# All low parts of a stage by accumulating transfers, and a third modulation computed as rows, in a two-layer trunk kernel

## Chip, core and metric

The kernel runs on one core of one Trainium2 chip. The metric is the device time of one execution in microseconds (us). Before the change three runs gave 1405.65, 1405.88 and 1407.29, median 1405.88. The execution whose trace is shown took 1407.28, and its span, from the first to the last instruction, is 1405.5.

The engines are called as the profile calls them: PE (TensorE, matmuls), DVE (VectorE), ACT (ScalarE), POOL (GpSimd) and SP (SyncE, which issues most transfers). Each works through its own list of instructions in a fixed order.

## What is computed

Two layers of a "hybrid gated parallel" block with width 1024 over 256 latent and 256 context tokens; layer 0 does both sets (512 columns), layer 1 only the latents, with keys and values of the context. In short:

```python
ml = silu(c) @ w_ada + b_ada          # six vectors of 1024: shift, scale, gate, shift, scale, gate
z  = modulate(x, ml[0], ml[1]) @ w_in + b_in
m  = sig(g0)*attention(q, k, v) + sig(g1)*conformer_conv(a) + sig(g2)*multiscale_pool(p)
x  = layer_norm(ALPHA*x + ml[2]*(m @ w_out + b_out))
x  = layer_norm(ALPHA*x + ml[5]*conv_ffn(modulate(x, ml[3], ml[4])))
```

`conformer_conv` is a gated linear unit, a depthwise convolution of 31 taps over the tokens, a layer norm, a silu and a pointwise matmul ("pw"). The vector `ml[2]` of layer 0, called modulation (0,2), is needed only behind the pointwise matmul, at `m @ w_out`.

## The kernel before

**Matmuls.** Activations lie with channels on partitions and tokens (512) in the free dimension. Each fp32 operand is split into a high part, rounded to the type fp32r, and a low part, the rest. Each product is three matmuls, high by high, low by high, high by low (lines 438, 439 and 440 of the program). One weight chunk (128 by 1024 fp32, 512 KB) gives eight slices of the contraction, so 24 matmuls of 512 columns into one accumulator bank. Four PSUM banks ("mm") are for these, three ("ax") for transposes and attention, one ("ad") for the modulation on PE.

**Weights.** They stream from memory in a fixed order, `ORDER`. SP loads a chunk into one of five buffers `raw`, or one of three buffers `rawt`. ACT copies it to `hi` (L290). The low part `lo` is made in one of two ways: DVE subtracts, `raw - hi` (L298), or, for the chunks in the list `SUMMED`, ACT writes minus `hi` into `lo` (L292) and POOL issues a transfer that adds the weights from memory to it (L294). Five chunks can be held as `hi` and `lo`. `SUMMED` holds every other chunk of layer 0's gates, pools and pointwise matmul, 22 of 44.

**Stages of layer 0.** Convolution inputs, keys and values, queries (two halves; the second half ends in four banks at once, which DVE empties into `nat` with the bias `bq`, L937), then sixteen steps of gates, pools, and attention heads spread over them, about 189 to 435 us; then the pointwise chunks. For each half of the queries DVE rotates `nat` to `rot` (POOL makes one part of it, `rotb`, and `rq`, the norm's factor), PE transposes, ACT and DVE split the result into `qThi` and `qTlo` (L449). A head's scores go through row maximum `mx` (L973), its product `nb`, exponential on ACT `p`, and PE transposes.

**Taps.** The depthwise convolution is 30 operations on DVE per block of channels (L796 on `H`), eight blocks. They are handed out in lots: `NTAPS` gives the lot for each phase (in the gate steps 10 in layer 0), and from step `FLUSH` on all that are left. They have a lower priority than other work. The finished `H` are transposed on PE (L505), their statistics taken, and normalized (`nat`, L529 and L533); after the gates they are transposed back (L544) and go through silu to `ch` and `clo`, the operands of the pointwise matmul.

**Modulations.** Two ways again. Kind "ada": PE multiplies eight chunks by `silu(c)` (L364, eight matmuls to a chunk as the trace counts them), DVE adds the bias (L371), and the row goes to memory. Kind "adt": the chunk lies in a `rawt` buffer, transposed, and DVE multiplies and sums it against the broadcast `silu(c)`, one pass for the latents and one for the context (L396), into a column of `mods`. A taken "adt" chunk is put on a list, `due`; `run_due(2)` at the end of each of the sixteen steps emits two. In layer 0's gates stage (0,2) is of the first kind, (0,4) and (0,3) of the second.

**Order.** A list scheduler, with a model of its own, orders each engine's instructions when the program is built. Where a line says `keep_in_program_order`, the instruction only stays behind the last such one of its engine. So the order that results is not that of the program text, and is shown below.

Of the kernel before, what the change touches and what calls it, by code (L numbers as in the profile page):

```python
# [7 lines left out]
F32 = mybir.dt.float32  # L8
# [5 lines left out]
P = 128  # L14
DEPTH = 2
D = 1024
KT = 8
# [24 lines left out]
NFF = 3  # L42
S3 = (1, 0)
PV3 = (0, 0)
FLUSH = (13, 14)
LATER = 1
HEAD_AT = (0, 1, 2, 4, 5, 7, 9, 10)
MIX_AT = 4
GRP = 3
GATES = ((0, 2), (0, 5), (1, 2), (1, 5))  # L50
TAPS_LATER = 60
NTAPS = ((10, 6, 10, 1000), (12, 7, 11, 1000))

_VEC = [
    ("b_in", 60), ("b_ada", 48), ("dw_b", 8), ("cln_g", 8), ("cln_b", 8), ("pw_b", 8),
# [8 lines left out]
NV = _o  # L64


_ADA = {(0, "mix"): ((0, 2),), (0, "up"): ((0, 5),), (1, "conv"): ((1, 2),), (1, "up"): ((1, 5),)}

_ADT = {(0, "mix"): ((0, 4), (0, 3)), (0, "up"): ((1, 1),), (0, "down"): ((1, 0), (1, 4), (1, 3))}

PRE = [("conv", 1, j, h) for j in range(8) for h in range(2)] + [("kv", 1, k) for k in range(4)]
PRE += [("q", 1, c, k) for c in range(2) for k in range(4)]
# [4 lines left out]
def _spread(main, extra):  # L77

    res, n = [], 0
    for i, x in enumerate(main):  # L80
        res.append(x)
        while n < len(extra) and n * len(main) < (i + 1) * len(extra):
            res.append(extra[n])
            n += 1
    return res


def weight_order(l):

    o = [("conv", l, j, h) for j in range(8) for h in range(2)]  # L90
    o += [("kv", l, k2) for k2 in range(4)]
    o += [("q", l, c, k2) for c in range(2) for k2 in range(4)]
    for n in range(16):
        b, i = (("g0", "g2", "pool")[n % 3], n // 3) if n < 12 else ("g1", n - 12)
        o += [(b, l, 2 * i), (b, l, 2 * i + 1)]
        if n >= MIX_AT and (n - MIX_AT) % 3 == 0 and n - MIX_AT < 12:
            o.append(("plw", l, (n - MIX_AT) // 3))
    o += [("pw", l, c) for c in range(8)]
    ada = {
        ph: [("ada", a, m, k) for a, m in _ADA.get((l, ph), ()) for k in range(KT)] for ph in ("mix", "conv", "up")  # L100
    }
    adt = {ph: [("adt", a, m, c) for a, m in _ADT.get((l, ph), ()) for c in range(KT)] for ph in ("mix", "up", "down")}

    o = o[:GRP] + ada["conv"] + o[GRP:20] + _spread(o[20:], _spread(ada["mix"], adt["mix"]) if l == 0 else [])
    o += [("wout", 0, h, p) for h in range(2) for p in range(4)] if l == 0 else [("wout", 1, k) for k in range(KT)]
    up = [("up", l, j, h) for j in range(FT) for h in range(2)]
    o += up[:GRP] + ada["up"] + _spread(up[GRP:], _spread([("pre",) + it for it in PRE if l == 0], adt["up"]))
    if l == 0:
        down = [("down", 0, h, p) for h in range(2) for p in range(FT // 2)]
        o += _spread(down[:-HOLD - 2], adt["down"]) + down[-HOLD - 2:]  # L110
    else:
        o += [("down", 1, k) for k in range(FT)]
    return o
# [23 lines left out]


SUMMED = [it for it in weight_order(0) if it[0] in ("g0", "g1", "g2", "pool", "plw", "pw")]
SUMMED = [it for i, it in enumerate(SUMMED) if i % 2]  # L140

OFFSET, _o = {}, 0
for _it in ORDER:
# [7 lines left out]
def trunk(ctx: ExitStack, tc: tile.TileContext, xT, xn, cT, crow, wst, vec, brow, grow, rows, bgate, rope, icnt, ident, out):  # L151
    nc = tc.nc
    V, A, G, PE, SP = nc.vector, nc.scalar, nc.gpsimd, nc.tensor, nc.sync
# [5 lines left out]
    dp = ctx.enter_context(tc.tile_pool(name="dp", bufs=1, space=bass.MemoryType.DRAM))  # L159
# [6 lines left out]
    def uid(name):  # L166
        cnt[0] += 1
        return f"{name}{cnt[0]}"
# [25 lines left out]
    def aux():  # L194
        return pax.tile([P, 512], F32, tag="ax", name=uid("ax"))

    def sm(w, name, bufs=None):
        return st.tile([P, w], F32, tag=f"sm_{name}", name=uid(name), bufs=bufs)
# [102 lines left out]
    def take(it):  # L301

        while True:
            i = nxt["use"]
            nxt["use"] += 1
            load_to(i + (LA0 if strict else LA))
            split_to(i if strict or only else ahead[i])
            if ORDER[i][0] not in ("ada", "adt", "pre") and unfinished:
                unfinished[0][0] -= 1
                if not unfinished[0][0]:  # L310
                    unfinished.pop(0)[1]()
            if ORDER[i] == it:
                return raw.pop(it) if it[0] == "ad0" else split.pop(it)
            if ORDER[i][0] == "ada":
                ada(*ORDER[i][1:])
            elif ORDER[i][0] in ("adt", "pre"):
                due.append(ORDER[i])
# [22 lines left out]
    mods = {}  # L340
    ada_ps = {}
    gate_row = {}
# [44 lines left out]
    def adt(l, m, c):  # L387

        w = raw.pop(("adt", l, m, c))
        n = 2 if l == 0 or m < 2 else 1  # L390
        if c == 0:
            mods[l, m] = const.tile([P, KT, 2], F32, name=f"mod{l}_{m}")
            if n == 1:
                G.memset(mods[l, m], 0.0)
        for s in range(n):
            tc.keep_in_program_order(V.tensor_tensor_reduce(  # L396
                prod, w, cb[:, s], 1.0, col(l, "b_ada", m * 8 + c), ALU.mult, ALU.add, mods[l, m][:, c, s:s + 1],
            ))

    def run_due(n):  # L400

        for _ in range(min(n, len(due))):
            it = due.pop(0)
            (adt if it[0] == "adt" else pre)(*it[1:])
# [75 lines left out]
    def mmB(w, src, T, ps=None, s=None):  # L480

        ps = mmb() if ps is None else ps
        a, b = (0, T) if s is None else (s * SEQ, (s + 1) * SEQ)
        mm3(ps[:, a:b], [(part(w, k * P, (k + 1) * P), part(src[k], a, b)) for k in range(len(src))])
        return ps
# [278 lines left out]
    for l in range(DEPTH):  # L764
# [278 lines left out]

        def gates(b, c):
            gate_end(b, c, mmB(take((f"g{b}", l, c)), hT, T))

        def gate_end(b, c, ps):
            g = ST(T, name=f"g{b}")
            A.activation(g[:, :T], ps[:, :T], AF.Sigmoid, bias=col(l, "b_in", 36 + 8 * b + c))
            gate[b, c] = g  # L1050
# [5 lines left out]
        def pooled(g):  # L1056
            w = 2 << g
            res = []
            for c2 in range(2):
                ps = mmB(take(("pool", l, 2 * g + c2)), hT, T)  # L1060
                u = mp.tile([P, 2, 272], F32, tag="pu", name=uid("pu"), bufs=2)
                V.memset(u[:, :ns, 0:8], 0.0)
                V.memset(u[:, :ns, 264:272], 0.0)
                A.activation(u[:, :ns, 8:264], v3(ps, ns), AF.Identity, bias=col(l, "b_in", 28 + 2 * g + c2))
                cur = u
                for lev in range(g + 1):
                    a = 1 << lev
                    nx = mp.tile([P, 2, 272], F32, tag="pl", name=uid("pl"), bufs=3)
                    lo, hi = a, 272 - (a if lev else 0)
                    sh0, sh1 = (-1, 0) if lev == 0 else (-a // 2, a // 2)  # L1070
                    V.tensor_tensor(
                        nx[:, :ns, lo:hi], cur[:, :ns, lo + sh0:hi + sh0], cur[:, :ns, lo + sh1:hi + sh1], op=ALU.add,
                    )
                    cur = nx

                o = ST(T, name="pooled")
                V.scalar_tensor_tensor(
                    v3(o, ns), cur[:, :ns, 8:264], 1.0 / w, u[:, :ns, 8:264], op0=ALU.mult, op1=ALU.subtract,
                )
                for s in range(ns):  # L1080
                    oe = o[:, half(s)].rearrange("p (e t) -> p e t", t=8)[:, ::31, :]
                    ce, ue = (x[:, s, 8:264].rearrange("p (e t) -> p e t", t=8)[:, ::31, :] for x in (cur, u))
                    V.tensor_tensor(oe, ce, ic[:, g], op=ALU.mult)
                    V.tensor_tensor(oe, oe, ue, op=ALU.subtract)
                res.append(hilo(o, T, "po"))
            return res
# [60 lines left out]
        for c in range(8):  # L1147
            ps = its[c][1] if c < GRP else mmB(take(("pw", l, c)), cT_, T)
            if l == 0:
                xres[c // 2].append(S(name="x"))  # L1150
                load(xres[c // 2][-1], xn[c // 2 * P:(c // 2 + 1) * P, c % 2 * 512:(c % 2 + 1) * 512], False)
            t = ST(T, name="pwo")
            V.scalar_tensor_tensor(
                t[:, :T], ps[:, :T], col(l, "pw_b", c), gate.pop((1, c))[:, :T], op0=ALU.add, op1=ALU.mult,
            )
            madd(c, t)
            mT.append(hilo(mt[c], T, "m"))
            run_due(len(due))
            if l == 1 and c == GRP:
                for h in range(2):  # L1160
                    V.tensor_tensor(ob[h], gates[0][h], ob[h], op=ALU.mult)
                    V.scalar_tensor_tensor(b[h], b[h], ALPHA, ob[h], op0=ALU.mult, op1=ALU.add)
                todo = r.scaled((0, 1), g, b)
            elif todo:
                todo.pop(0)()
# [232 lines left out]
```

## Time and profile before

| | |
|---|---|
| median of three runs | 1405.88 us (1405.65 to 1407.29) |
| the profiled execution | 1407.28 us, span 1405.5 us |
| PE busy | 1366.1 us, 97% |
| DVE, ACT, POOL busy | 1101.8, 715.7, 88.7 us |
| DMA | 276.23 MB; software queue 11.01 MB, 4.4% of 16 engines' span |
| gate steps | about 189 to 435 us |

In the views, a timeline row is start, duration, engine, line, operation, output<-inputs, shape, count, and in brackets the idle time before it with what ended it. Durations of neighbouring instructions overlap, so what one costs is read from start to start. A row by stretch gives the length, then busy time (and count) of PE, PE's weight loads, DVE, ACT and POOL, the granted clock of PE (1.00 is full), the busy share of the DMA engines and GB/s. A row of waits gives engine, line, what was waited for, total us, times, longest.

### The profile page before, as it was taken

What the parts mean: (1) busy time and instruction counts of PE and PEld (TensorE: products, weight loads), DVE (VectorE), ACT (ScalarE), POOL (GpSimd) and SP (SyncE); (2) the same over time, 40 slices, a digit from 0 to 9 for tenths busy, and PEclk for the clock granted to TensorE, in tenths of its full rate; (3) what the DMA queues carried; (4) which work ended last, traced back from release to release, by engine and by line L of the source; (5) the groups of instructions that cost most, each with busy time, mean ns of one, the idle gap of its engine ahead of it and who ended that gap; (6) DMA issues with size and microseconds to landing.
All of it is one profiled execution on the core that took longest, in us unless ns stands there. A gap on an engine that the chain in (4) does not pass through costs nothing.

```text
span 1405.5 us, 20642 instructions
## 1 busy us (share of the span) xinstructions
PE 1366.1 (97%) x7764; PEld 1164.0 (83%) x7764; DVE 1101.8 (78%) x1959; ACT 715.7 (51%) x1136; POOL 88.7 (6%) x87
## 2 busy tenths in 40 slices
PE   7999999999998999999999999999999999899997
PEld 5788877888887888888888888798889998799986
DVE  3498997996995887788776787479889969787755
ACT  3432557765847414544544321253687774555550
POOL 0020530000001000000000000010500000000000
PEclk9999999999999999999999999999999999999999
DMA  9634455356464736577676797597623365755560
GB/s 346 222 114 142 150 128 165 99 153 175 113 186 130 222 118 227 208 254 257 235 253 213 250 320 258 210 348 287 249 96 128 113 210 200 281 184 183 186 216 30
DMA packets 83957, 276.23 MB, mean 197 GB/s; under 512 B 9593, under 2 KB 10257, under 8 KB 83729
## 3 DMA queue, kind: packets, MB, share of 16 engines
q1 hardware_dynamic: 79968, 263.03, 54.0%
q0 software_dynamic: 3168, 11.01, 4.4%
q8 instruction: 61, 1.00, 0.3%
q10 hardware_dynamic: 720, 0.87, 0.2%
q14 instruction: 40, 0.32, 0.1%
HBM read 259.12 MB, written 15.75 MB: 196 GB/s over the span
## 4 chain that ended last, share of the span: by engine, by line
PE 79%; DVE 12%; ACT 2%; issue 1%; DMA 1%; POOL 0%; POOLq 0%; DVEq 0%; ACTq 0%
PE mm L438 24%; PE mm L439 24%; PE mm L440 24%; DVE H L796 6%; PE ax L472 3%; DVE lo L298 2%; PE ax L1011 1%; DMA raw<-in_wst 1%; PE ad L364 1%; PE ax L583 1%; DVE gl L820 0%; PE ax L438 0%; PE ax L439 0%; PE ax L440 0%; ACT hi L290 0%
## 5 line engine op out<-in xcount | busy, mean ns | idle before, releaser
L290 ACT ACTIVATE hi<-raw 128x1024 fp32r<-128x1024 f32 (+1 forms) x223 | 230.8, 1043 | 303.5 <-PE mm L439 109.4
L438 PE MATMUL mm<-hh,hi 128*128 128x256 f32 (+1 forms) x1112 | 349.1, 318 | 2.2 <-DVE acc L1230 1.0
L439 PE MATMUL mm<-hl,hi 128*128 128x256 f32 (+1 forms) x1112 | 350.5, 316 | 0.4 <-DVE hl L603 0.4
L440 PE MATMUL mm<-hh,lo 128*128 128x256 f32 (+1 forms) x1112 | 349.3, 315 | 0.0
L298 DVE TENSOR_TENSOR lo<-raw,hi 128x1024 fp32r<-128x1024 f32 (+1 forms) x184 | 220.6, 1203 | 80.0 <-ACT hi L290 77.9
L796 DVE SCALAR_TENSOR_TENSOR H<-gl,vt,H 128x245 f32<-128x245 f32 (+29 forms) x480 | 267.4, 609 | 1.9 <-ACT H L788 1.6
L438 PEld LDWEIGHTS mm<-hh,hi 128*128 128x128 f32 x1112 | 211.2, 192 | 16.9 <-DVE gl L820 1.3
L439 PEld LDWEIGHTS mm<-hl,hi 128*128 128x128 f32 x1112 | 212.4, 191 | 15.0 <-issue 1.4
L440 PEld LDWEIGHTS mm<-hh,lo 128*128 128x128 f32 x1112 | 212.4, 191 | 14.6 <-issue 1.7
L438 PE MATMUL mm<-hi,hi 128*128 128x512 f32 x464 | 184.3, 397 | 2.0 <-DVE nat L937 1.0
L440 PE MATMUL mm<-hi,lo 128*128 128x512 f32 x368 | 144.4, 392 | 1.6 <-DVE lo L298 1.6
L439 PE MATMUL mm<-xlo,hi 128*128 128x512 f32 x368 | 144.3, 392 | 0.2 <-DVE xlo L713 0.2
L396 DVE CUSTOM_DVE_ANT_0 prod<-rawt,cb,vt 128x1024 f32<-128x1024 f32 x80 | 102.3, 1279 | 6.1 <-DMA rawt<-in_wst 4.9
L438 PEld LDWEIGHTS mm<-hi,hi 128*128 128x128 f32 x464 | 87.2, 188 | 23.7 <-issue 3.9
L290 ACT ACTIVATE hi<-rawt 128x1024 fp32r<-128x1024 f32 x62 | 65.2, 1059 | 68.7 <-PE mm L440 26.2
L438 PE MATMUL mm<-hi,ah 128*128 128x512 f32 x252 | 98.1, 390 | 0.0
L439 PE MATMUL mm<-lo,ah 128*128 128x512 f32 x252 | 98.1, 389 | 0.0
L440 PE MATMUL mm<-hi,al 128*128 128x512 f32 x252 | 97.9, 389 | 0.0
L298 DVE TENSOR_TENSOR lo<-rawt,hi 128x1024 fp32r<-128x1024 f32 x51 | 62.7, 1231 | 26.8 <-ACT hi L290 26.2
L440 PEld LDWEIGHTS mm<-hi,lo 128*128 128x128 f32 x368 | 69.1, 188 | 17.2 <-DVE lo L298 2.9
L439 PEld LDWEIGHTS mm<-xlo,hi 128*128 128x128 f32 x368 | 69.2, 188 | 13.9 <-DVE xlo L713 0.5
L438 PEld LDWEIGHTS mm<-hi,ah 128*128 128x128 f32 x252 | 47.3, 188 | 10.3 <-DVE acc L1237 0.3
(222 smaller groups left out, 2190.2 us busy)
## 6 DMA issues: line engine op xcount, KB each, us to landing
raw<-in_wst SPq DMA_DIRECT2D x247, 512.0 KB, 4.7
rawt<-in_wst SPq DMA_DIRECT2D x145, 512.0 KB, 4.8
scr<-rawt SPq DMA_DIRECT2D x28, 512.0 KB, 3.7
lo<-scr SPq DMA_DIRECT2D x28, 512.0 KB, 5.3
lo<-in_wst POOLq DMA_DIRECT2D x20, 512.0 KB, 7.8
ad<-in_wst SPq DMA_DIRECT2D x32, 256.0 KB, 6.0
prow<-in_rows SPq DMA_DIRECT2D x20, 256.0 KB, 7.0
gate<-grow SPq DMA_DIRECT2D x12, 256.0 KB, 6.5
```

What stands on the lines that cost most here:

```text
L290: pin(A.activation(hi[:, :w], r[:, :w], AF.Copy))
L298: pin(V.tensor_tensor(lo[:, :w], r[:, :w], hi[:, :w].bitcast(F32), op=ALU.subtract))
L364: PE.matmul(ps[32 * j:32 * j + 32, :], sc[:, k, :], w[:, j * 256:(j + 1) * 256], start=(k == 0), stop=(k == KT - 1),)
L396: tc.keep_in_program_order(V.tensor_tensor_reduce(prod, w, cb[:, s], 1.0, col(l, "b_ada", m * 8 + c), ALU.mult, ALU.add, mods[l, m][:, c, ...
L438: pin(PE.matmul(ps, lh, rh, start=(first and i == 0), stop=False))
L439: pin(PE.matmul(ps, lh, rl, start=False, stop=False))
L440: pin(PE.matmul(ps, ll, rh, start=False, stop=(last and i == n - 1)))
L472: PE.matmul(ps, x[:, a:b], y[:, c:d], start=(i == 0), stop=(i == n - 1))
L583: PE.transpose(a[:, c2 * 256 + tt * P:c2 * 256 + (tt + 1) * P], self.res[2 * s + tt][i // 2][:, o:o + P], ID,)
L796: V.scalar_tensor_tensor(h[:, :, a:b], g[:, :, a + d:b + d], col(l, "dw_w", k * 8 + j), h[:, :, a:b], op0=ALU.mult, op1=ALU.add,)
L1011: PE.transpose(t_ps[:, kt * 256 + q2 * P:kt * 256 + (q2 + 1) * P], p[:, o:o + P], ID)
```

## The change

1. `SUMMED` holds all 44 chunks: no low part of these is subtracted on DVE any more.
2. Modulation (0,2) becomes of the kind "adt", ahead of (0,4) and (0,3); its bias load as a gate row is gone. A new function `rows_of` transposes its columns on PE behind the second pointwise chunk, copies and writes the rows to memory, where the gate reads them as before.
3. `run_due(2)` is also called behind each gate and each pool matmul.
4. Lots of taps in the gate steps are 12 instead of 10, and all that are left are handed out from step 12 instead of 13.

```diff
-FLUSH = (13, 14)
+FLUSH = (12, 14)
-GATES = ((0, 2), (0, 5), (1, 2), (1, 5))
+GATES = ((0, 5), (1, 2), (1, 5))
-NTAPS = ((10, 6, 10, 1000), (12, 7, 11, 1000))
+NTAPS = ((10, 6, 12, 1000), (12, 7, 11, 1000))
-_ADA = {(0, "mix"): ((0, 2),), (0, "up"): ((0, 5),), (1, "conv"): ((1, 2),), (1, "up"): ((1, 5),)}
-_ADT = {(0, "mix"): ((0, 4), (0, 3)), (0, "up"): ((1, 1),), (0, "down"): ((1, 0), (1, 4), (1, 3))}
+_ADA = { (0, "up"): ((0, 5),), (1, "conv"): ((1, 2),), (1, "up"): ((1, 5),)}
+_ADT = {(0, "mix"): ((0, 2), (0, 4), (0, 3)), (0, "up"): ((1, 1),), (0, "down"): ((1, 0), (1, 4), (1, 3))}
-    o = o[:GRP] + ada["conv"] + o[GRP:20] + _spread(o[20:], _spread(ada["mix"], adt["mix"]) if l == 0 else [])
+    o = o[:GRP] + ada["conv"] + o[GRP:20] + _spread(o[20:], adt["mix"])
-SUMMED = [it for i, it in enumerate(SUMMED) if i % 2]
+    def rows_of(l, m):
+        pt = aux()
+        PE.transpose(pt[:2 * KT, :P], mods[l, m].rearrange("p k s -> p (k s)"), ID)
+        row = sm(256, "adarow", bufs=1)
+        V.tensor_copy(row[:2 * KT, :P], pt[:2 * KT, :P])
+        gate_row[l, m] = dp.tile([2, D], F32, name=uid("grow"))
+        for s in range(2):
+            load(
+                gate_row[l, m][s:s + 1, :].rearrange("o (k x) -> (o k) x", k=KT),
+                row[:2 * KT, :P].rearrange("(k s) x -> k s x", s=2)[:, s, :], False,
+            )
...
         def gates(b, c):
             gate_end(b, c, mmB(take((f"g{b}", l, c)), hT, T))
+            run_due(2)
...
                 ps = mmB(take(("pool", l, 2 * g + c2)), hT, T)
+                run_due(2)
...
             run_due(len(due))
+            if l == 0 and c == 1:
+                rows_of(0, 2)
```

Line numbers after the change are 12 higher from `run_due` on, and one lower ahead of `rows_of`.

Three places show how the change moves instructions. First DVE, between the split of the last transposed queries (`qTlo`) and the emptying of the banks of the second half of the queries (`nat`). Before:

```order
L449 TENSOR_TENSOR qTlo195_1631<-ax193_1624,qThi194_1629 128x512
L449 TENSOR_TENSOR qTlo198_1640<-ax196_1633,qThi197_1638 128x512
L937 TENSOR_TENSOR nat199_1666<-mm183_1497,bq182_1495 128x512
L937 TENSOR_TENSOR nat200_1667<-mm184_1498,bq182_1495 128x512
L796 SCALAR_TENSOR_TENSOR H126_1081<-gl95_660,vt0_82,H126_1081 128x2x249
L937 TENSOR_TENSOR nat201_1668<-mm185_1499,bq182_1495 128x512
```

In the changed kernel (`prod, mod0_2` are the passes of modulation (0,2); rows with `mod0_2` alone are their read-outs):

```order
L461 TENSOR_TENSOR qTlo196_1631<-ax194_1624,qThi195_1629 128x512
L395 ISA prod_92,mod0_2_1769<-rawt61_943,cb_91,vt0_82 128x1024
...
L395 ISA prod_92,mod0_2_1769<-rawt64_1094,cb_91,vt0_82 128x1024
...
L985 TENSOR_REDUCE mx225_1819<-ax223_1814 128x1
L395 ISA prod_92,mod0_2_1769<-rawt67_1184,cb_91,vt0_82 128x1024
...
L985 TENSOR_REDUCE mx237_1850<-ax235_1842 128x1
L395 ISA prod_92,mod0_2_1769<-rawt70_1306,cb_91,vt0_82 128x1024
...
L949 TENSOR_TENSOR nat197_1657<-mm181_1490,bq180_1488 128x512
```

Six passes (two each for `rawt64` and `rawt67`, one each for `rawt61` and `rawt70`), three row maxima of head 0 with their products, and three taps now stand between `qTlo196` and `nat197`; one pass more stands ahead of the two `qTlo`. On PE the scores of head 0 (`ax223`, `ax229`, `ax235`), which stood behind the first two gate chunks, now stand right behind the last query matmul and ahead of the first gate matmul, `mm219`, which takes the bank of `nat197`.

Second, SP's queue of loads around the bias `bq` of those banks, before:

```order
L218 DMA raw75_1531<-in_wst 128x1024
L218 DMA raw77_1563<-in_wst 128x1024
L218 DMA bq182_1495<-in_brow 128x512
L218 DMA raw78_1612<-in_wst 128x1024
L218 DMA raw79_1618<-in_wst 128x1024
```

and in the changed kernel:

```order
L217 DMA raw84_1916<-in_wst 128x1024
L217 DMA rawt70_1306<-in_wst 128x1024
L217 DMA raw85_1918<-in_wst 128x1024
L217 DMA rawt73_1368<-in_wst 128x1024
L217 DMA bq180_1488<-in_brow 128x512
```

The load `rawt70` takes the buffer of `rawt61`, and `rawt73` that of `rawt64`: each is issued when the second pass over the older one is done, and `bq180` is behind both.

Third, ACT ahead of the pointwise stage, before (`nat` are the norm's, `lo129` a negated copy):

```order
L529 ACTIVATE nat282_2053<-nat282_2053,nm618_4036,lrs617_4033 128x256 x2
L529 ACTIVATE nat604_3899<-nat604_3899,nm618_4036,lrs617_4033 128x256 x2
L292 ACTIVATE lo129_4190<-raw129_3976 128x1024
L1039 ACT_TABLE_LOAD
L1039 ACTIVATE ch622_4089<-ax620_4079,vt0_82 128x256
```

and in the changed kernel:

```order
L541 ACTIVATE nat594_3804<-nat594_3804,nm616_4041,lrs615_4038 128x256 x2
L291 ACTIVATE lo128_4054<-raw128_3945 128x1024
L289 ACTIVATE hi129_4193<-raw129_3979 128x1024
L1062 ACTIVATE g1608_4013<-mm607_3988,vt0_82 128x512
L291 ACTIVATE lo129_4194<-raw129_3979 128x1024
L289 ACTIVATE hi131_4201<-raw131_4051 128x1024
L1051 ACT_TABLE_LOAD
L1051 ACTIVATE ch620_4093<-ax618_4083,vt0_82 128x256
```

The last norm has moved ahead of a gate's sigmoid (`g1608`); between it and the table load stand more weight copies. On PE the transposes that feed this norm (L505, now L517) end 102 rows ahead of the back-transposes (L544, now L556) instead of 31.

## The prediction

> **What bounds the kernel now.** I read first the engine table of the page, then the waits of TensorE (PE) in the stretch that the change touches, 180 to 470 us, then busy time by stretch.
>
> ```profile
> PE 1366.1 (97%) x7764; PEld 1164.0 (83%) x7764; DVE 1101.8 (78%) x1959; ACT 715.7 (51%) x1136; POOL 88.7 (6%) x87
> ...
> PE mm L438 <- ACT ch L1039: 2.9, 1, 2.9
> PE ax L438 <- ACT pT L462: 1.6, 1, 1.6
> PE mm L438 <- DVE nat L937: 1.0, 1, 1.0
> PE mm L439 <- DVE clo L449: 0.7, 1, 0.7
> ...
> 180.00:190.00 10.00, 8.95 (x49) 6.66 (x48) 10.00 (x16) 4.73 (x10) 1.75 (x3) 1.00 0.79 210
> 220.00:428.00 208.00, 208.00 (x1016) 170.01 (x1015) 184.58 (x377) 130.38 (x208) 13.11 (x15) 1.00 0.54 151
> 440.00:450.00 10.00, 9.33 (x41) 7.23 (x42) 3.99 (x5) 8.29 (x18) 0.00 (x0) 0.83 0.68 194
> ```
>
> PE is busy 1366 of 1405.5 us. In the gate and pool stage (the row 220 to 428: length, PE, weight loads, DVE, ACT, POOL, granted clock, DMA share) it never stops. Work taken off VectorE (DVE) there buys nothing by itself: a gain can come only from PE work removed, or from the four waits above. At 180 to 190 the rows say something else: DVE is busy 10.00 of 10, and PE waits for it once (nat L937). That is the place where the change adds DVE work, and the forecast rests on it.
>
> **The handover from queries to gates.** All four accumulators ("mm") hold the second half of the queries until DVE has added the bias into `nat`; the first gate matmul needs one of them. Before:
>
> ```profile
> 187.19 1.28 DVE L449 TENSOR_TENSOR qTlo<-ax,qThi 128x512 fp32r<-128x512 f32 x2
> 188.39 1.27 DVE L937 TENSOR_TENSOR nat<-mm,bq 128x512 f32<-128x512 f32 x2
> ...
> 181.03 0.64 PE L364 MATMUL ad<-raw,sc 128*32 128x256 f32 x8
> 181.60 1.09 PE L928 MATMUL ax<-ID,rot 128*128 128x128 f32 x8
> 187.78 0.39 PE L440 MATMUL mm<-hi,xlo 128*128 128x512 f32 x1
> 189.22 0.47 PE L438 MATMUL mm<-hi,hi 128*128 128x512 f32 x1 [1.05 <-DVE nat L937]
> 200.22 0.39 PE L438 MATMUL ax<-kThi,qThi 128*128 128x512 f32 x1
> 202.29 0.40 PE L438 MATMUL mm<-hi,hi 128*128 128x512 f32 x1
> ```
>
> The eviction begins the moment `qTlo` ends, and PE loses 1.05 us. In the changed order DVE has, between the last `qTlo` and the first `nat`, six modulation passes, three row maxima with their three small products, and three taps. Their prices:
>
> ```profile
> 426.41 1.27 DVE L396 CUSTOM_DVE_ANT_0 prod<-rawt,cb,vt 128x1024 f32<-128x1024 f32 x1
> 427.62 0.08 DVE L396 DVE_READ_ACCUMULATOR2_ANT mod<- 128x1 f32 x1
> 198.45 5.21 DVE L796 SCALAR_TENSOR_TENSOR H<-gl,vt,H 128x496 f32<-128x496 f32 x8
> 203.59 1.27 DVE L973 TENSOR_REDUCE mx<-ax 128x1 f32<-128x512 f32 x2
> 204.79 0.14 DVE L974 TENSOR_TENSOR nb<-mx,rq 128x1 f32<-128x1 f32 x1
> 204.85 0.41 DVE L973 TENSOR_REDUCE mx<-ax 128x1 f32<-128x256 f32 x1
> ```
>
> A pass takes 427.62 - 426.41 = 1.21 us from start to start, its read-out hides under the next start: six are 7.26. Maxima: (204.79 - 203.59)/2 = 0.60 twice and about 0.35 for the half-size one: 1.55. Products: 0.06 each, 0.2. Taps: 5.21/8 = 0.65 each, 1.95. Together 11.0 us. With DVE at the end of `qTlo` at the same 188.39, the first `nat` starts at 199.4 instead of 188.39, and PE's first gate matmul at 189.22 + 11.0 = 200.2.
>
> What PE has meanwhile: its last query matmul starts at 187.78; two modulation chunks of 181.60 - 181.03 = 0.57 are gone ahead of it, so it is done near 186.9; and the scores of head 0, which stood behind two gate chunks (202.29 - 200.22 = 2.07 us), now stand ahead of the first gate and run at once. PE is out of work near 188.9 and stands until 200.2. Of these 11.0 us of lateness 2.07 is repaid because the scores are done: **+9.0**. The two removed chunks are swallowed by the wait. Bounds: DVE could reach `qTlo` earlier, since two `lo` subtractions before it (1.2 us each by the page's 1203 ns row) are gone; against that the POOL queue now has an accumulating transfer and one `rq` ahead of the second `rotb`, for which DVE's `rot` waits, 1 us or 2. So 8 to 10.
>
> A second thing arrives at the same time. The bias `bq` for `nat` is now issued by SP behind two loads into `rawt` buffers, the later of which waits until the fourth of these passes is done.
>
> ```profile
> DMA to landing us min/median/max: 5.3/5.3/5.3
> ```
>
> That pass ends near 188.39 + 4 x 1.21 + 2 x 0.65 less the one pass that stood ahead of `qTlo`: three passes and two taps, 4.9 us, 193.3. A `bq` issued at about 194 lands at 199.3, when DVE wants it (199.4). At a busy time of the DMA engines (share 0.79 above) it may be 2 us later: the upper bound is 11. What is late next is head 0's probabilities: its transposes wait perhaps 1.5 to 2 us where before head 0 cost PE the 1.62 us on `pT`; I take +0.3.
>
> A stop of PE also costs clock. The row 440 to 450 shows 0.83 of the clock behind the wait of 2.88 us:
>
> ```profile
> 442.02 0.63 PE L440 MATMUL mm<-ch,lo 128*128 128x512 f32 x1
> 442.45 0.63 PE L439 MATMUL mm<-clo,hi 128*128 128x512 f32 x1
> ...
> 210.00:220.00 10.00, 8.38 (x46) 6.88 (x45) 9.79 (x19) 9.69 (x15) 0.88 (x1) 1.00 0.44 113
> 1200.00:1210.00 10.00, 6.53 (x38) 5.89 (x39) 8.19 (x18) 5.57 (x9) 0.56 (x1) 0.66 0.99 368
> ```
>
> Matmuls start 0.43 apart there instead of 0.23, and 0.17 of 10 us is 1.7 us lost. After the 1.62 us wait (210 to 220) nothing is lost; in the worst stretch (1200 to 1210) 0.34 of 6.5 busy us, 2.2. A wait of 11 us is far beyond 2.88: **+1.7**, bounds 0 and 2.2. The Trainium skill ("TensorE: Matmul & The Clock Gate", What's actually happening) says that the clock halves after an idle window of about 3.4 us and comes back after as long a busy one. By it, as an estimate, an 11 us stop costs 3.4/2 = 1.7 us too, but a stop under 3.4 us nothing; the trace does not bear out so sharp a limit: 2.88 us of waiting gave 0.83.
>
> **PE work removed.** Modulation (0,2) leaves PE: eight chunks. Two lie ahead of the wait above, the eighth in the gap below (436.37, where PE waits anyway); five count, 5 x 0.57 = **-2.9**. The transposition that replaces its rows is one 128-column matmul at 1.40/12 = 0.12 (first row below): +0.1. The sixteen DVE passes beyond the wait lie under PE: before, DVE had 184.6 of 208 us there; of the change's 22 removed subtractions some 20 lie there (-24 us by 1203 ns), against nine more passes (+11 us). If that cover were gone each would cost its 1.21.
>
> **The gap before the pointwise stage.**
>
> ```profile
> 434.97 1.47 PE L544 MATMUL ax<-ID,nat 128*128 128x128 f32 x12
> 436.37 0.64 PE L364 MATMUL ad<-raw,sc 128*32 128x256 f32 x8
> 439.89 0.96 PE L438 MATMUL mm<-ch,hi 128*128 128x512 f32 x3 [2.88 <-ACT ch L1039]
> ...
> 436.46 1.04 ACT L292 ACTIVATE lo<-raw 128x1024 fp32r<-128x1024 f32 x1
> 437.52 1.28 ACT L1039 ACT_TABLE_LOAD   x1
> 438.81 1.02 ACT L1039 ACTIVATE ch<-ax,vt 128x256 fp32r<-128x256 f32 x2
> ```
>
> The gates end at 434.97 on PE; ACT is then still normalizing, until 436.46, and one weight copy, the table load and `ch` follow. With taps in larger lots the feed of the norm stands 102 PE rows ahead of the back-transposes instead of 31, so the norm is over before the gates end. What stays behind the last gate is a weight copy (1.04; its buffer comes free with that gate), the load 1.28 and `ch` 1.02. The chain starts at about 435.4 instead of 436.46: **-1.1**, bounds 0 and -2.9 (the whole wait). The idle stays near 3 us, so its clock loss stays too.
>
> **Accumulating transfers.** 22 subtractions go; in their place come 22 negated copies on ACT, 22 issues on POOL and 11 MB on the software queue.
>
> ```profile
> L292 ACT ACTIVATE lo<-raw 128x1024 fp32r<-128x1024 f32 (+1 forms) x22 | 22.3, 1013 | 4.0 <-PE mm L439 4.0
> L294 POOL DMA_DIRECT2D lo<-in_wst x22 | 19.5, 888 | 247.6 <-ACT lo L292 109.6 <-DVE H L796 54.9 <-DVE nb L974 26.0
> lo<-in_wst POOLq DMA_DIRECT2D x20, 512.0 KB, 7.8
> q0 software_dynamic: 3168, 11.01, 4.4%
> ```
>
> ACT goes from 130 to about 150 of 208 us, POOL stays idle. A low part is ready 1.0 + 0.9 + 7.8 = 9.7 us behind its high part, against 1.2 before; a chunk feeds PE for 24 x 0.227 = 5.4 us and five chunks have buffers, so there are some 10 us left. The queue's 4.4% of 1405 us is 62 us; as much again over about 270 us lifts the DMA share from 0.54 to 0.77. I take 0, above it the last rival.
>
> **Sum**, against the profiled execution's own 1407.28: 9.0 + 0.3 + 1.7 - 2.9 + 0.1 - 1.1 = +7.1, 1414.4. The median of the runs is 1.4 below that execution, so **1413.0**; with the bounds of the terms 1409 to 1417.
>
> **Rivals.**
> 1. Faster: the wait does not arise, because DVE is so far ahead at `qTlo` that the passes are done by the time the accumulators fill. Then seven chunks count: -4.0 - 1.1 + 0.1 = -5.0, **1400.9**. For it: subtractions leave DVE, and PE is the bound. Against it: DVE is busy 10.00 of 10 at 180 to 190 and was late already by 1.05; it would have to gain 11 us and loses two subtractions.
> 2. About the same: half of it. If DVE comes 5 us earlier to `qTlo`, the term is 4.0 and the clock loss small: 4.0 + 0.3 + 0.5 - 2.9 + 0.1 - 1.1 = +0.9, **1406.8**; with the whole gap before the pointwise stage gone too, 1405.0.
> 3. Worse: the transfers. `bq` 2 us late, and low parts later than PE wants them: if one in four of 22 is 1 us late, 5 us; 7.1 + 2 + 3 to 5 = **1418 to 1420**. It decides when landing goes from 7.8 to over some 18 us. For it: share 0.77. Against: no wait of PE on a transferred low part before.
>
> **How the numbers follow.** Forecast 0.60, rival 1 0.18, rival 2 0.12, rival 3 0.10. The range from 1402 to 1418 leaves out most of rival 1 and half of rival 3. The likeliest case's own range is 1409 to 1417. About 0.2% (2.8 us) is what a measurement of this kernel can tell from no change. Slower takes the forecast, rival 3 and little of rival 2: 0.71; same 0.11; faster 0.18.
>
> **What would show it.** Right: one PE wait of 9 to 12 us near 190 on `nat`, first gate matmul at 199 to 202, on DVE six passes of L395 between `qTlo` and `nat`; a granted clock near 0.8 in the ten us behind it; no L364 chunk between 190 and 440; the wait on `ch` 2 to 3 us; no wait on `lo`. Wrong: `nat` at once behind `qTlo` or PE at the gates before 195 (rivals 1, 2); many short waits at the third product of a chunk (rival 3). If the wait is there but `nat` stood ready with DVE idle, `bq` was the cause and not the passes.

## The result and the profile after

The changed kernel took **1427.87 us** (median of four runs, 1425.07 to 1429.36) against 1405.83 before: a ratio of 1.0152, 95% interval 1.0132 to 1.0172, slower by 22 us. The forecast was slower, 1413, with 1402 to 1418 as its range: the direction is right, the size is not, and of the two stops described below one was not forecast. The profiled execution of the changed kernel has a span of 1427.1 us.

The waits of PE over the whole span, and two stretches of ten us, are the first things to read:

```profile
PE mm L450 <- DVE nat L949: 11.6, 2, 11.3
PE mm L450 <- ACT ch L1051: 6.4, 1, 6.4
PE mm L452 <- DMA lo<-in_wst: 5.7, 5, 1.8
PE ax L556 <- DVE nat L545: 5.5, 1, 5.5
...
200.00:210.00 10.00, 10.00 (x39) 8.18 (x39) 10.00 (x19) 7.14 (x35) 9.26 (x9) 0.86 0.15 49
450.00:460.00 10.00, 2.87 (x10) 2.33 (x11) 1.45 (x5) 9.66 (x15) 0.99 (x2) 0.50 0.85 181
460.00:470.00 10.00, 10.00 (x41) 7.76 (x41) 2.77 (x4) 7.72 (x16) 0.92 (x2) 0.72 0.64 161
```

There are two stops. The first, 11.3 us on `nat`, is the one that was forecast (11.3 us of standing from 188.9 to 200.2). The second lies around the end of the gates and was not: PE waits for low parts, for the norm (L545) and for `ch` (6.4 us where before it waited 2.88), and the clock is at 0.50 and 0.72 there.

**Where the time went.** The rows are the last gate matmul before the change, then the first gate matmul, the last gate matmul and the first pointwise matmul after it:

```profile
434.74 0.39 PE L440 MATMUL mm<-hi,lo 128*128 128x512 f32 x1
...
199.71 0.80 PE L450 MATMUL mm<-hi,hi 128*128 128x512 f32 x1 [11.29 <-DVE nat L949]
444.37 0.39 PE L452 MATMUL mm<-hi,lo 128*128 128x512 f32 x1
459.12 1.65 PE L450 MATMUL mm<-ch,hi 128*128 128x512 f32 x3 [6.39 <-ACT ch L1051]
```

From the last high-by-low gate matmul to the first pointwise matmul PE needed 434.74 to 439.89 before, 5.2 us, and 444.37 to 459.12 after, 14.8: 9.6 us more. From there to the first `wout` matmul it was 48.5 before and 51.9 after, 3.3 us more. Up to that last gate matmul the changed kernel is 9.6 us later (444.37 against 434.74), although it entered the stage 2.3 us earlier (last query matmul at 185.53 against 187.78). Together 9.6 + 9.6 + 3.3 = 22.5; later stages give about 1 back.

**The first stop** on DVE, in the timeline of the changed kernel:

```profile
186.00 1.28 DVE L461 TENSOR_TENSOR qTlo<-ax,qThi 128x512 fp32r<-128x512 f32 x2
...
198.96 2.49 DVE L949 TENSOR_TENSOR nat<-mm,bq 128x512 f32<-128x512 f32 x4 [0.76 <-DMA bq<-in_brow]
```

From 187.21, where the work behind `qTlo` begins, to `nat` it is 11.75 us; the forecast had 11.0 of DVE work, and 0.76 was a wait for the bias, as its bound allowed.

**The second stop** begins on POOL. The factor of the norm, `lrs`, is a small operation there, and it stands behind the accumulating transfers that POOL issues:

```profile
407.10 0.87 POOL L293 DMA_DIRECT2D lo<-in_wst  x1 [4.85 <-issue]
411.34 0.86 POOL L293 DMA_DIRECT2D lo<-in_wst  x1 [3.37 <-ACT lo L291]
420.79 0.89 POOL L293 DMA_DIRECT2D lo<-in_wst  x1 [8.59 <-ACT hi L289]
428.39 0.87 POOL L293 DMA_DIRECT2D lo<-in_wst  x1 [6.71 <-issue]
434.13 0.89 POOL L293 DMA_DIRECT2D lo<-in_wst  x1 [4.87 <-issue]
434.70 1.05 POOL L532 TENSOR_TENSOR lrs<-ve,mhalf 128x2 f32<-128x2 f32 x1
...
435.78 0.16 DVE L534 SCALAR_TENSOR_TENSOR nm<-mv,lrs 128x2 f32<-128x2 f32 x1 [12.86 <-POOL lrs L532]
435.98 1.09 ACT L541 ACTIVATE nat<-nat,nm,lrs 128x256 f32<-128x256 f32 x2 [15.12 <-DVE nm L534]
420.52 0.50 PE L452 MATMUL mm<-hi,lo 128*128 128x512 f32 x1 [1.35 <-DMA lo<-in_wst]
428.12 0.50 PE L452 MATMUL mm<-hi,lo 128*128 128x512 f32 x1 [1.85 <-DMA lo<-in_wst]
```

The word "issue" is what matters: POOL stands 4.85, 6.71 and 4.87 us ahead of an issue, and nothing that the program orders explains it. ACT had written the negated copy for the transfer issued at 428.39 by 411.3. DVE then waits 12.86 us for `lrs`, ACT 15.12 us for DVE, and behind ACT's norm stand the copies of the next chunks. What POOL waits for shows in the packets of the software queue, listed here from the records of the same trace (issue on POOL; first packet; end of the last packet; us):

```
issue 407.10  first 408.69  last 410.70
issue 411.34  first 414.88  last 419.94
issue 420.79  first 423.93  last 427.77
issue 428.39  first 429.98  last 433.52
issue 434.13  first 435.73  last 439.13
issue 439.74  first 444.32  last 447.79
```

Each issue comes 0.6 to 0.9 us after the last packet of the transfer before it. It is so for 34 of the 43 issues that follow another (within 0.8 us), and in none of the 43 is a packet of an earlier transfer unfinished. The queue holds one 512 KB transfer at a time: 0.6 us or more, then 1.6 us or more to the first packet, then the data, 2.0 us at the least and 3.7 in the median of the 44. Where it is full an issue follows an issue after 6.5 us (median). While heads are spread over the gates a chunk comes more slowly than that, every 6.9 us (ACT wrote 28 negated copies between 209.3 and 402.5); behind the last head PE needs 24 x 0.227 = 5.4 for one, and the queue falls behind: the transfer issued at 439.74 is 18.9 us later than its copy.

### The profile page after: what moved, and what is told of

Same layout as the page of the kernel before. It is cut to its first block, busy times and chain, and to the rows that moved or that the text cites. A ratio compares the mean times of both kernels' runs of the same rounds, so it can differ in the third digit from the quotient of the medians.

```text
span 1427.1 us, 20565 instructions
## 1 busy us (share of the span) xinstructions
PE 1366.1 (96%) x7701; PEld 1167.0 (82%) x7701; DVE 1093.9 (77%) x1969; ACT 736.5 (52%) x1160; POOL 106.2 (7%) x109
## 4 chain that ended last, share of the span: by engine, by line
PE 77%; DVE 9%; DMA 3%; issue 3%; ACT 2%; POOL 1%; POOLq 0%; SPq 0%; DVEq 0%; ACTq 0%
PE mm L450 23%; PE mm L451 23%; PE mm L452 23%; DVE H L808 4%; PE ax L484 3%; PE ax L1023 1%; DVE lo L297 1%; DMA lo<-in_wst 1%; DMA bq<-in_brow 1%; DMA raw<-in_wst 1%; DMA x<-in_xn 1%; ACT hi L289 1%; PE ax L595 1%; DVE prod L395 0%; PE ax L450 0%
## 5 line engine op out<-in xcount | busy, mean ns | idle before, releaser
L289 ACT ACTIVATE hi<-raw 128x1024 fp32r<-128x1024 f32 (+1 forms) x226 | 234.1, 1044 | 306.1 <-PE mm L451 115.3
L808 DVE SCALAR_TENSOR_TENSOR H<-gl,vt,H 128x482 f32<-128x482 f32 (+29 forms) x480 | 268.3, 609 | 1.9 <-ACT H L800 1.5
L297 DVE TENSOR_TENSOR lo<-raw,hi 128x1024 fp32r<-128x1024 f32 (+1 forms) x165 | 198.5, 1209 | 71.1 <-ACT hi L289 70.3
L395 DVE CUSTOM_DVE_ANT_0 prod<-rawt,cb,vt 128x1024 f32<-128x1024 f32 x96 | 122.9, 1280 | 4.6 <-DMA rawt<-in_wst 3.9
L289 ACT ACTIVATE hi<-rawt 128x1024 fp32r<-128x1024 f32 x59 | 61.9, 1059 | 55.8 <-PE mm L452 26.6
L297 DVE TENSOR_TENSOR lo<-rawt,hi 128x1024 fp32r<-128x1024 f32 x48 | 59.2, 1234 | 27.0 <-ACT hi L289 27.0
L578 POOL TENSOR_TENSOR lrs<-ve,mhalf 128x1 f32<-128x1 f32 x12 | 8.6, 716 | 682.6 <-DVE ve L577 682.6
```

The costliest lines, as they stand in the source:

```text
L289: pin(A.activation(hi[:, :w], r[:, :w], AF.Copy))
L297: pin(V.tensor_tensor(lo[:, :w], r[:, :w], hi[:, :w].bitcast(F32), op=ALU.subtract))
L395: tc.keep_in_program_order(V.tensor_tensor_reduce(prod, w, cb[:, s], 1.0, col(l, "b_ada", m * 8 + c), ALU.mult, ALU.add, mods[l, m][:, c, ...
L578: G.tensor_tensor(rs, ve, mhalf[:, :1], op=ALU.pow)
L808: V.scalar_tensor_tensor(h[:, :, a:b], g[:, :, a + d:b + d], col(l, "dw_w", k * 8 + j), h[:, :, a:b], op0=ALU.mult, op1=ALU.add,)
```

## Experiments

All ratios are against the kernel before, measured on the same chip beside the experiments; its median was 1405.29 us beside e1 to e4, 1404.84 beside e5 to e8 and 1406.25 beside e9 to e12. The texts set off below are what was expected before each run.

### Which part makes which stop

**e1, the bias load untied.** A load on SP is tied, unless its call says otherwise, behind the load issued before it. The load of `bq` thereby stood behind `rawt73`, whose buffer comes free only when the second pass over `rawt64` is done, so no order could put `nat` ahead of the passes over `rawt61` and `rawt64`.

```diff
-            load(bq, brow[l:l + 1, boff:boff + 512].to_broadcast([P, 512]))
+            load(bq, brow[l:l + 1, boff:boff + 512].to_broadcast([P, 512]), False)
```

> The changed kernel with one argument altered: the bias load of the queries is no longer tied behind the loads issued before it. Theory T (two causes, one at the queries and one at the accumulating transfers): the six modulation passes and the bias load behind two modulation chunks cause the 11.3 us wait before the first gate; it falls to about 1 us, with the clock loss behind it. The second stop, before the pointwise stage (waits on the norm 5.5, on ch 6.4, on low parts 5.7 us), stays. So 1414 to 1419 us. Rival R (the transfer queue alone sets the end, the first wait only gives it time): the wait moves into waits on low parts, 1424 to 1428 us. Rival S (the wait at the queries is DVE's load of passes and not the order of loads): the wait stays above 8 us, 1425 or more.

Measured: **1422.08 us**, ratio 1.0113 (1.0096 to 1.0130). The waits of PE:

```profile
PE mm L452 <- DMA lo<-in_wst: 7.0, 5, 2.3
PE mm L450 <- ACT ch L1051: 6.4, 1, 6.4
PE ax L556 <- DVE nat L545: 4.9, 1, 4.9
PE mm L450 <- DVE nat L949: 2.4, 2, 2.1
```

The first stop is gone, 11.3 to 2.1 us: the tie made it, and rival S falls. In the order that results, `nat` stands right behind `qTlo` again, with the same passes later. But only 5 us of it reach the end (+16.8 us against +22.0), between what T and R expected: the waits on low parts grew from 5.7 to 7.0, and a part of what was gained is spent on the queue.

**e2, every other chunk by transfer again.**

```diff
 SUMMED = [it for it in weight_order(0) if it[0] in ("g0", "g1", "g2", "pool", "plw", "pw")]
+SUMMED = [it for i, it in enumerate(SUMMED) if i % 2]
```

> The changed kernel with accumulating transfers for every other chunk again (22 instead of 44), all else changed. Theory T: the wait before the first gate stays at about 11 us, the waits on low parts and on the norm before the pointwise stage go (ch at most 3 us): 1411 to 1416 us, which is what the prediction summed. Rival U (the late norm comes from larger lots of taps, from the earlier flush and from modulation passes on DVE and ACT, not from the transfers): the stop before the pointwise stage stays above 8 us, 1422 or more.

Measured: **1411.93 us**, ratio 1.0045 (1.0029 to 1.0062). The waits:

```profile
PE mm L451 <- DVE nat L950: 12.0, 1, 12.0
PE mm L451 <- ACT ch L1052: 1.9, 1, 1.9
PE mm L453 <- DVE lo L298: 1.1, 1, 1.1
```

The first stop stays, the second is gone, and no wait on a transferred low part is left. Rival U falls: lots of taps, the earlier flush and the modulation passes are all still in this kernel. Its +6.6 us are near the forecast's sum (+7.1), but e2 keeps 22 subtractions on DVE that the sum took as gone; e5 below, without them, is the closer test of it.

**e3, both.** The edits of e1 and e2 together.

> Both: bias load untied and 22 transfers. Theory T: neither stop; what is left is the modulation taken off TensorE, seven chunks of 0.57 us, and the shorter gap before the pointwise stage: 1399 to 1403 us, faster than before. Rival U: 1410 or more.

Measured: **1402.47 us**, ratio 0.9978 (0.9963 to 0.9993): as expected, a little faster than before. The waits on `nat` and `ch` are 1.5 and 1.9 us.

**e4, the kernel before with 44 transfers.**

```diff
-SUMMED = [it for i, it in enumerate(SUMMED) if i % 2]
```

> The kernel before with nothing changed but that all 44 chunks take their low parts by accumulating transfers. Theory T: the first wait stays at 1 us as before; the queue takes one transfer at a time, some 6 us each against 5.4 us of TensorE work to a chunk, falls behind, and the norm's factor stands behind it on GpSimd: 1413 to 1420 us. Rival U: 1404 to 1407 us, waits as before.

Measured: **1427.17 us**, ratio 1.0150 (1.0119 to 1.0180). The waits:

```profile
PE ax L543 <- DVE nat L532: 11.1, 2, 8.9
PE mm L439 <- DMA lo<-in_wst: 5.4, 4, 2.3
PE mm L437 <- ACT ch L1038: 2.9, 1, 2.9
PE mm L437 <- DVE nat L936: 1.9, 1, 1.9
```

This one part of the change, alone, costs as much as the whole. It is more than theory T expected; the rival is out. The two stops do not quite add. Counted from e3, where both are absent (-2.8 us against before), the first alone costs 9.5 us (e2), the second alone 19.6 (e1), and both 24.9 (the changed kernel), not 29.1. That the queue catches up while PE stands at the first stop would explain this; no run tries it apart.

### The queue

**e5, each transfer in two halves.** The same bytes, 64 partitions at a time.

```diff
-                G.dma_start(lo[:, :w], wst[o:o + P * w].rearrange("(p c) -> p c", p=P), accum_op=ALU.add)
+                for b in range(0, P, 64):
+                    G.dma_start(
+                        lo[b:b + 64, :w], wst[o:o + P * w].rearrange("(p c) -> p c", p=P)[b:b + 64], accum_op=ALU.add,
+                    )
```

> The changed kernel with each accumulating transfer issued as two, of 64 partitions each: the same bytes, twice as many transfers of half as many packets (72 instead of 144). If the software queue takes one transfer at a time (an issue only after the last packet of the one before, 0.6 us, and 1.6 us until the first packet), a half costs about 0.6 + 1.6 + 2 = 4.2 us and a chunk 8.4 instead of 6.2: more than 1450 us, and in the trace no two halves overlap. If the limit is one of packets or bytes in flight, the two halves of a chunk overlap, a chunk still costs about 6.2 us and the time stays at 1422 to 1432.

Measured: **1407.81 us** (one run; before 1404.84). Its waits and a piece of its POOL timeline:

```profile
PE mm L453 <- DVE nat L952: 12.0, 2, 11.7
PE mm L453 <- ACT ch L1054: 1.9, 1, 1.9
...
319.10 1.65 POOL L294 DMA_DIRECT2D lo<-in_wst  x2 [14.02 <-ACT lo L291]
320.99 0.81 POOL L294 DMA_DIRECT2D lo<-in_wst  x1 [0.24 <-issue]
323.42 0.81 POOL L294 DMA_DIRECT2D lo<-in_wst  x1 [1.62 <-issue]
```

and the packets of these four halves, 80 to each, from the same records (shared out in the order of their start):

```
issue 319.10  first 320.69  last 323.52
issue 319.64  first 322.64  last 326.30
issue 320.99  first 325.89  last 328.03
issue 323.42  first 327.77  last 330.65
```

If one transfer at a time were a rule of numbers, halves would cost 8.4 us a chunk and the time would pass 1450. They overlap: at 320.99 two earlier halves are unfinished. Call a transfer live from its issue until it has landed. At 65 of the 88 issues three are live, the one issued among them, and never four. The 1.6 us ahead of the first packet is then hidden behind the data of the one before, and 19 us are gone: with the first stop still whole (11.7 us), +3.0 us is left of +22.0. So the second stop is the queue that holds one whole transfer.

**e6, the norm's factor off POOL.** From e1; a square root on ACT and a reciprocal on DVE stand in for the power on POOL.

```diff
-            G.tensor_tensor(rs, ve, mhalf[:, :2], op=ALU.pow)
+            A.activation(rs, ve, AF.Sqrt)
+            V.reciprocal(rs, rs)
```

> The kernel with the bias load untied and all 44 transfers, with the norm's factor (two small operations before the pointwise stage) taken from GpSimd: a square root on ScalarE and a reciprocal on VectorE in its place, with its table loads. Theory H (the factor stands behind queued transfers on GpSimd, and this is most of the second stop): the waits on the norm (4.9 us) and most of that on ch (6.4 us) go, the waits on low parts stay or grow: 1408 to 1416 us. Theory Q (the rate of the queue alone sets the end of the gates and of the pointwise stage): what is gained at the norm is lost again on low parts, 1418 or more.

Measured: **1419.98 us**, ratio 1.0112 (1.0088 to 1.0136), 2 us less than e1:

```profile
PE mm L452 <- DMA lo<-in_wst: 12.7, 6, 5.9
...
PE mm L450 <- ACT ch L1052: 2.8, 2, 1.9
```

The wait on the norm goes and that on `ch` before the pointwise stage falls from 6.4 to 1.9, as theory H said, and the time comes back on low parts, 7.0 to 12.7, as theory Q said. The place behind the queue is where the stop shows; the rate of the queue is its cause.

**e7, 36 transfers.** From e1; every other chunk of gate 1 and of the pointwise matmul is subtracted on DVE.

```diff
+SUMMED = [it for i, it in enumerate(SUMMED) if i % 2 or it[0] not in ("g1", "pw")]
```

> The bias load untied, and 36 transfers: all of the gates 0 and 2, pools and plw, every other one of gate 1 and of the pointwise chunks. The queue is over-full only from about 370 us on, and its backlog is 15 us at the norm; with 8 transfers fewer in the last stretch it is not behind there. Theory T: no stop before the pointwise stage, 1399 to 1405 us, as with 22 transfers. Rival: the queue is behind already in the first gates, waits on low parts of 3 us or more remain, 1408 or more.

Measured: **1401.38 us**, ratio 0.9979 (0.9968 to 0.9991). No wait on a transferred low part is left, and `ch` is at 1.9 us. So the queue carries the chunks of the stretch with the heads, and is too slow behind them, where chunks follow each other at 5.4 us.

**e8, old lots of taps.** From e3, with `FLUSH = (13, 14)` and 10 instead of 12.

> The bias load untied, 22 transfers, and taps in the old lots (10, all from step 13). If the larger lots move the norm off the path as the prediction said, the wait on ch comes back from 1.9 to about 3 us and the time rises by 1 to 2 us, 1403 to 1405. If they do nothing, 1402 as with them.

Measured: **1402.38 us**, ratio 0.9978 (0.9967 to 0.9989): the same as e3. The norm is later and PE waits 3.7 us for it (not for `ch`, as expected), so that the gap before the pointwise stage is 6.7 us against 3.6 in e3. But the gates take 2.9 us less: in e3, with the larger lots, PE waits there 1.1 us for the taps (`H`) and 1.2 for their statistics (`bst`), in e8 for neither. The larger lots are worth nothing that can be measured here.

### Both stops away

**e9, the bias load untied and transfers in halves**, the edits of e1 and e5 in the changed kernel.

> The changed kernel with both stops taken away and all 44 chunks by accumulating transfers: the bias load untied, and each transfer issued as two halves of 64 partitions. Theory T (the two stops are the tied bias load and the software queue that holds one whole transfer at a time): neither stop, no wait on low parts: 1398 to 1403 us, faster than before. Rival: with VectorE relieved and the queue fuller, waits on low parts come back when the first stop no longer gives the queue time: 1408 or more.

Measured: **1399.98 us**, ratio 0.9949 (0.9934 to 0.9965), faster than both kernels, and with e12 the fastest of all:

```profile
PE mm L453 <- DVE nat L952: 2.4, 2, 2.1
PE mm L453 <- ACT ch L1054: 1.9, 1, 1.9
...
220.00:428.00 208.00, 208.00 (x999) 172.90 (x998) 183.34 (x403) 152.31 (x239) 52.64 (x64) 1.00 0.78 187
```

PE works through 220 to 428 without a gap, with the DMA engines at 0.78 and ACT at 152 of 208 us, near the 0.77 and 150 of the forecast. The same row of e3, where the other 22 subtractions are on DVE:

```profile
220.00:428.00 208.00, 205.27 (x986) 170.78 (x985) 202.98 (x425) 139.81 (x222) 16.52 (x18) 1.00 0.57 152
```

DVE is at 203 of 208 us there instead of 183, and PE has gaps. e9 gains 6.3 us on before and e3 2.8; with the first stop in place it is the same, +3.0 in e5 and +6.6 in e2. In both pairs the kernel with all 44 low parts by halves is about 3.5 us faster than the one with 22 whole transfers.

**e10, the kernel before with 44 transfers in halves**: e4 with the edit of e5.

> The kernel before with all 44 chunks by transfers (as in the run that took 1427) and each transfer as two halves, nothing else changed. Theory T: the whole 20 us of that run were the one-at-a-time queue, so the time is that of the kernel before within a few us, 1402 to 1408. Rival (the load on the DMA engines or on ScalarE, 22 more copies, is what costs): 1415 or more.

Measured: **1411.87 us**, ratio 1.0041 (1.0027 to 1.0054): 16 of e4's 22 us are gone, 6 are left, between the two expectations. The longest wait that is left in this stretch is on `ch`:

```profile
PE mm L440 <- ACT ch L1041: 5.1, 1, 5.1
...
432.89 0.81 POOL L294 DMA_DIRECT2D lo<-in_wst  x1 [1.87 <-issue]
433.43 1.00 POOL L522 TENSOR_TENSOR lrs<-ve,mhalf 128x2 f32<-128x2 f32 x1
...
429.14 0.17 DVE L521 TENSOR_SCALAR ve<-mv 128x2 f32<-128x2 f32 x1
434.46 0.16 DVE L524 SCALAR_TENSOR_TENSOR nm<-mv,lrs 128x2 f32<-128x2 f32 x1 [3.59 <-POOL lrs L522]
```

`lrs` was ready to run at 429.3 and ran at 433.4, behind halves that POOL could not yet issue. In the changed kernel the norm is asked for earlier relative to the gates, and the same 4 us are hidden. That is argued from these rows and was not tried apart. The wait on `ch` is 2.2 us longer than before the change; what else makes up the 6 us is not shown.

**e11, quarters**: e9 with 32 partitions at a time. (The "first run" in this text and the next is e9.)

> As the first run of this call, but each transfer as four quarters of 32 partitions. If the queue is limited by packets (halves of 80 packets showed at most 160 unfinished at an issue, wholes of 144 none), up to five quarters are in flight; if by the number of transfers, at most three. Time 1398 to 1408 us, unless 176 issues of 0.9 us on GpSimd hold it up.

Measured: **1407.53 us** (one run; before 1406.25). Up to six quarters are live (at 88 of 176 issues), as a rule three halves, one whole: not a rule of numbers, and not one of packets alone either (six quarters are 288 packets, as many as two wholes, which never overlap). What the unit of the limit is stays open. The quarters gain nothing: 176 issues keep POOL longer, and PE waits 4.7 us on `ch`.

**e12, without handing out passes behind each gate and pool matmul**: e9 less the two added calls.

```diff
-            run_due(2)
```

> As the first run of this call without the calls that hand out two modulation passes behind each gate and pool matmul (only at the end of each step, as before). Theory T: those calls cost nothing and gain nothing by themselves, TensorE is the bound: within 3 us of the first run. If the passes are too late without them (24 of them at two per step, and loads behind them), the time rises by 3 us or more.

Measured: **1399.72 us**, ratio 0.9956 (0.9940 to 0.9972), the same as e9: these calls of `run_due` do nothing for the time that can be measured.

## Why the prediction was right in direction and wrong on the transfers

**What bounds the kernel: right, with one part left out.** In e9, where both stops are gone, the gain is 6.3 us, near the 5.0 that the first rival worked out for seven modulation chunks off PE and the shorter gap. The prediction said that work taken off DVE buys nothing by itself, and named the 22 subtractions that go as the cover for the new passes. As cover they count: with those subtractions still on DVE (e3 against e9, e2 against e5) the change is worth about 3.5 us less.

**The handover from queries to gates: right in place and size.** 11.0 us of DVE work forecast, 11.75 from `qTlo` to `nat` measured; PE's standing 11.3 forecast, 11.3 measured. In time the stop is worth 9.5 us with its clock (e2 against e3), where the forecast and its first rival, which has no stop, lie 12.1 apart. One point in it was weighed wrongly: I took the passes as the cause and the bias load as a second thing that arrives at the same time. It is the reverse. The load's tie forced passes ahead of `nat`, and untying it moved the first two `nat` right behind `qTlo` (e1) with no pass removed.

**Clock: right in the changed kernel, but not a fixed price.** +1.7 forecast; the ten us behind the first stop have 0.86, 1.4 us. In e2, with the same stop (12.0 us), they have 0.72, 2.8 us, above the upper bound of 2.2.

**The gap before the pointwise stage: the gap right without the queue, wrong with it.** In e2 it is 442.07 to 445.72, 3.6 us against 5.2 before, so -1.5 for a forecast of -1.1. But e8 shows that the larger lots, which were to bring it, gain no time: what the gap loses the gates take. In the changed kernel the gap was +9.6. My step read the order of ACT and PE there, and took no account of `lrs` on POOL, which was in the order too, behind transfers.

**Accumulating transfers: the step that failed.** "I take 0" rested on 9.7 us from a high part to its low part and five buffers: a latency with room. That is a statement on one transfer. What was needed was a rate: how often can the queue deliver? It delivers one chunk in 6.5 us (median) where it is full, against 5.4 that PE needs behind the last head. The transfers did not become slower (6.5 us to landing in the median, before 7.8), so the third rival's condition, landing above 18 us, was never met, and yet its mechanism happened. Measured in place of the 0: 22 us alone (e4), 16 us on top of the first stop (1427.87 against e2's 1411.93, which differs by this alone). Nor did "POOL stays idle" hold: it is busy little, but it stands at issues, and what stands behind them waits.

The trace of before had the sign. Three of its 21 issues that follow another came 0.65 to 0.87 us after the last packet of that transfer; the rest came later and found the queue empty, since issues were 12 us apart in the median. With twice the transfers that spacing was bound to meet the 6.5. I read the mean share of the DMA engines (0.54 to 0.77, and e9 shows that they bear it) and not the queue's own spacing.

By the Trainium skill ("DMA: Bandwidth & Descriptors", Anatomy of one DMA — SWDGE (gpsimd) path) a transfer issued from GpSimd takes a fixed 2.0 us and its bytes at 436 GB/s, an estimate of 3.2 us for 512 KB, at which the queue would have kept up. The trace does not agree: 5.8 us in the median from issue to last packet of an accumulating one, 2.6 us over the estimate.

**Chances.** Slower had 0.71, and the transfer rival 0.10 with 1418 to 1420. The range's upper end was set by half of that rival; its price, "one in four late by 1 us", had no row behind it. That the change would be slower was not luck, since the first stop is there with about the size forecast, but it is less than half of the 22 us. That e2's +6.6 agrees with the sum of +7.1 is in part luck: with all 44 low parts off DVE and no second stop (e5, one run) it is +3.0, so the sum without the transfers was some 4 us too high.

## What to carry to other kernels

For work that moves to a queue, ask for its rate as well as its latency: the time from one issue to the next when the queue is full. Compare it with the time in which the consumer uses one item where it is fastest, not on average. Look at what else stands on the issuing engine, since a transfer that cannot be issued yet holds up every small operation behind it. And when a load is tied behind others, a wait of one of those for its buffer becomes a wait of whatever needs the load: here it forced VectorE's order.

## What the runs showed of the hardware

- An accumulating transfer of 512 KB issued from GpSimd is never issued while another is unfinished: 0 of 43 issues in the changed kernel, 34 of them within 0.8 us of the last packet of the one before, and 0 of 291 in the nine kernels with whole transfers. Two halves of 64 partitions overlap, with three live at most issues (65 of 88 in e5); of quarters up to six are live.
- From an issue to the first packet it takes 1.6 us or more, and the data of 512 KB another 2.0 or more, 3.7 in the median (all 44 of the changed kernel). Halves hide the first behind the data of the one before, worth 19 us here (+22.0 against +3.0 in e5, one run).
- POOL stands while a transfer cannot be issued, and a small operation behind it stands too: `lrs` was ready at 417.6 and ran at 434.70, with POOL busy 7% of the span.
- No run gives a length of wait at which PE's clock begins to suffer. Over the ten us behind a wait of 2.9 us (before) it was 0.83, behind 11.3 us 0.86 and behind 12.0 (e2) 0.72. Behind the 1.9 us on `ch` it was 0.83 in e2, e3 and e12 and 1.00 in e7 and e9.
